# Three more pairs' first products ahead of the first feed-forward, zero matmuls in the mixer, and another order of the mixer

## The chip, the cores and the metric

The kernel runs on one core of a Trainium2 chip. The metric is the device time of one execution in microseconds, the median of several runs. Five engines take part: TensorE (PE in the profile) multiplies, VectorE (DVE), ScalarE (ACT) and GpSimd (POOL) do the elementwise work, and SyncE (SP) issues nearly all DMAs, in order.

## The reference, cut to what matters

One layer of a decoder over 1024 positions of width 1024, in float32:

```
x = x + 0.5 * swiglu(rms_norm(x), w_gate1, w_up1, w_down1)      # D_FF = 2816
h = rms_norm(x);  p = h @ w_in                                  # all columns in one projection
    8 RWKV-7 heads of 64 (token shift, decay, in-context rate, state update, group norm, gate)
    4 pooling groups of 128 (trailing means over 2, 4, 8, 16 positions, a linear map each)
x = x + concat(y_rwkv, y_pool) @ w_out
x = x + 0.5 * swiglu(rms_norm(x), w_gate2, w_up2, w_down2)
out = rms_norm(x)
```

with `swiglu(x) = (silu(x @ w_gate) * (x @ w_up)) @ w_down`.

## The kernel before, in words

**Products.** Every operand of a matmul is split into a rounded high part and a low remainder, and a product is three matmuls (`mm3`, L251 to L254: high by high, high by low, low by high), 512 columns each. One product of two 512-deep blocks is 4 steps of `mm3`, so 12 matmuls. Splitting a weight block costs one ScalarE copy (the high part) and one VectorE subtraction (the low part).

**The first feed-forward.** The gate and up projections are done as 2 by 2 blocks by a Strassen scheme with seven products P1 to P7. The 22 tiles of the inner dimension f are taken in 11 pairs. For each pair and each of the two weights (gate, up) the products P1 and P2 need only two of the seven right-hand forms, `b11` and `b21`, which are the two upper-half blocks of the normalised x itself; the others need the sums `t1` to `t4` and `b22`.

**`start` (L699 on)** is the stretch before the main loop. A planner orders it: `inputs1` loads x, transposes it, normalises it and builds all the forms, most of it on VectorE, and meanwhile PE does P1 and P2 of the first `NPRE = 3` pairs, whose sums stay in SBUF. An `aside` argument names further pairs: for these `start` also computes P1, writes it to a DRAM tile, adds P2 to it, and writes the sum to DRAM as well (L788 to L798). In this kernel only the second feed-forward passes it (pairs 8 to 10; pairs 3 to 7 of the second feed-forward are computed in the mixer, by `begin`, L1713 to L1743).

**`gate_up` (L334 on)** is the main loop over 11 pairs: it loads both 512 KB halves of a pair's weights, does what products are left, applies silu, and stores the forms of the result that the down projection wants. For a pair that was put aside it does not do P1 and P2 but loads the two kept tiles (`kept`, L443 to L448). Which pairs those are is told by `a_left`: none in the first feed-forward, all but the first three in the second.

**The mixer** (L1070 to L1909) is one list of operations for all five engines: the columns of the combined projection, eight units (four head pairs by two halves of the sequence), the pooling groups, the output projection, the norms, and `begin`. Each operation has a modelled duration and its dependences. `Plan.emit` (L95 to L169) walks through it: at each step every engine offers the operation that could start first, ties are broken by rank (the longest way to the end, plus a number per part of the list from the table `LEAD`), and what starts first is emitted. The five instruction streams that come out are final; at run time each engine goes through its stream in order and waits on semaphores. The planner knows nothing of TensorE's clock. `start` and the down projections are planned in the same way, with the same `LEAD` table.

Of the kernel before, what the change touches and what calls it, by code (L numbers as in the profile page):

```python
# [16 lines left out]
P = 128  # L17
# [5 lines left out]
HT = 512  # L23
# [12 lines left out]
class Plan:  # L36
# [51 lines left out]
    def emit(self, lead):  # L88
# [28 lines left out]
        for i in range(n):  # L117
            if not waits[i]:
                queue.setdefault(self.ops[i][0], []).append(i)
        log = []  # L120
        dense = port = 0.0
        self.span = 0.0
        while any(queue.values()):
            best = None
            for eng, q in queue.items():
                cand = []
                for i in q:
                    s = max(ready[i], clock.get(eng, 0.0) + self.turn(prev.get(eng), i), port if self.ops[i][12] else 0.0)
                    need = {}
                    for t, g in self.ops[i][4]:  # L130
                        need[g] = need.get(g, 0) + 1
                    for g, c in need.items():
                        s = max(s, sorted(free[g])[c - 1] if len(free[g]) >= c else 1e9)
                    cand.append((s, i))
                if not cand:
                    continue
                s, i = min(cand, key=lambda c: (c[0], -rank[c[1]]))
                if s > 1e8:
                    continue
                if eng == "PE" and not self.full(i) and s + self.ops[i][1] > dense + self.THIN:  # L140

                    s, i = min([c for c in cand if self.full(c[1]) and c[0] <= s + self.WAIT] or [(s, i)],
                               key=lambda c: (c[0], -rank[c[1]]))
                if best is None or s < best[0]:
                    best = (s, i, eng)
            assert best is not None, "the tiles do not suffice"
            s, i, eng = best
            _, time, fn, _, new, lat, *_ = self.ops[i]
            queue[eng].remove(i)
            end = s + time  # L150
            self.span = max(self.span, end + self.ops[i][9])
            clock[eng] = end
            prev[eng] = i
            if self.full(i):
                dense = end
            if self.ops[i][12]:
                port = max(port, end)
            for t, g in new:
                free[g].remove(min(free[g]))
            for t in tile_of.get(i, ()):  # L160
                left[t] -= 1
                ends[t] = max(ends.get(t, 0.0), end + lat)
                if not left[t] and t in tag_of:
                    free[tag_of[t]].append(ends[t])
            for u in users[i] + after[i]:
                ready[u] = max(ready[u], s if u in after[i] else end + self.lag(i, u))
                waits[u] -= 1
                if not waits[u]:
                    queue.setdefault(self.ops[u][0], []).append(u)  # L169
            log.append((s, i))  # L170
            fn()

    THIN, WAIT = 1.8, 0.2

    def full(self, i):

        return self.ops[i][0] == "PE" and self.ops[i][1] in (0.45, 0.7, 0.86)
# [7 lines left out]
    def lag(self, i, u):  # L185
# [4 lines left out]

LEAD = {"": 48.5, "1e00": 696.8, "1e01": 905.5, "1e10": -2683.6, "1e11": 2081.2, "1e20": -2679.1, "1e21": -2658.5,
# [15 lines left out]

MANUAL = {mybir.EngineType.PE, mybir.EngineType.DVE, mybir.EngineType.Activation, mybir.EngineType.Pool,  # L210
          mybir.EngineType.SP}
# [3 lines left out]
def block_kernel(ctx, tc, x, ffn1_norm, ffn1_w_gate, ffn1_w_up, ffn1_w_down, mix_norm, w_in,  # L215
# [27 lines left out]
    def split(hi, lo, src, hi_eng="act", lo_eng="dve"):  # L243
# [4 lines left out]
        eng = nc.vector if lo_eng == "dve" else nc.gpsimd  # L248
        eng.tensor_tensor(lo, src, hi.bitcast(F32), op=ALU.subtract)  # L249

    def mm3(acc, lhi, llo, rhi, rlo, first, last):  # L251
        nc.tensor.matmul(acc, lhsT=lhi, rhs=rhi, start=first, stop=False)  # L252
        nc.tensor.matmul(acc, lhsT=lhi, rhs=rlo, start=False, stop=False)  # L253
        nc.tensor.matmul(acc, lhsT=llo, rhs=rhi, start=False, stop=last)  # L254

    ident = const.tile([P, P], F32, name="ident")
    make_identity(nc, ident)
# [65 lines left out]
    NPRE = 3  # L323

    NEARLY = 5
    PROD = ("P1", "P2", "P4", "P6", "P7", "P5", "P3")
    PROD2 = ("P1", "P2", "P3", "P6", "P7", "P5", "P4")

# [2 lines left out]

    def gate_up(fp, rf, begun, wg, wu, ascr, a_left, ahead):  # L334

# [115 lines left out]
        for i in range(NF // 2):  # L451
            ahead(i)
            qs = []
            for n, src in enumerate((wg, wu)):
                a = loads(src, i) if i + n else blocks
                if (i, n) in early:
                    c1, q = early[i, n], []
                elif a_left:
                    c1, q = kept(0, i, n), [kept(1, i, n)]
                else:  # L460
                    c1, c11 = first(a)
# [234 lines left out]
        return rb  # L696


    def start(fp, rf, wg, wu, ascr, inputs, pre, through, aside=()):  # L699

# [136 lines left out]
    x_v = x[0].rearrange("(i p) d -> p i d", p=P)  # L837
    xtd = dram.tile([NH, P, KD, HT], F32, name="xtd")
    x1d = dram.tile([NH, P, KD, HT], F32, name="x1d")
    ascr = dram.tile([7, NF // 2, P, HT], F32, name="ascr")  # L840

    DSC = 4 * (16 * L + 16)
# [12 lines left out]
    with tc.tile_pool(name="f12", bufs=2, side="right", reuse_waits="tile") as fp:  # L855
# [62 lines left out]
                    else:  # L918
                        rest_ops(k, a, b, "xn0" if k == 0 else "")

        begun = start(fp, right, ffn1_w_gate[0], ffn1_w_up[0], ascr, inputs1, "1", {"PE": 4.4, "ACT": 5.8})

        wb = w_blocks(lambda n: xb.tile([P, 8 * HT], F32, tag="x", name="wx") if n == 0 else xtile("wx", [P, 8 * HT]),
                      ffn1_w_down[0], False)
# [3 lines left out]
        def mixer_consts():  # L928
# [6 lines left out]
            nc.vector.tensor_scalar(hw[:, 4:8], vt[:, vc["a0"]:vc["a0"] + 4], 0.5, None, ALU.mult)  # L935
            nc.vector.tensor_scalar(hw[:, 8:12], vt[:, vc["ka"]:vc["ka"] + 4], 0.5, None, ALU.mult)
            nc.vector.tensor_scalar(hw[:, 12:16], vt[:, vc["ka"]:vc["ka"] + 4], -0.5, 1.0, ALU.mult, ALU.add)
            reset = const.tile([P, HT], BF16, name="reset")
            nc.vector.memset(reset, 1.0)
            nc.vector.memset(reset.rearrange("p (c l) -> p c l", l=L)[:, :, 0:1], 0.0)  # L940
            inv16 = const.tile([P, 4, 16], F32, name="inv16")
# [15 lines left out]
                for q in range(3):  # L957
                    load_a(fp, 0, q, PROD)

        gate_up(fp, rf, begun, ffn1_w_gate[0], ffn1_w_up[0], ascr, False, ahead1)  # L960

        hs2 = []

# [60 lines left out]
    xbs.close()  # L1024

    x2d = dram.tile([P, KD, HT], F32, name="x2d")
    c1d = dram.tile([2, NF // 2, 2, P, HT], F32, name="c1d")
    x2n = dram.tile([NH, P, 4, D], F32, name="x2n")
    with tc.tile_pool(name="mix", bufs=1, side="right", reuse_waits="tile") as mp_:

# [29 lines left out]
        def product(name, src, c0, n, rhs, reads, r="", over="", less=0, twice=False):  # L1060


            for j in range(2):
# [39 lines left out]
                for k in range(kn):  # L1103
                    def mm(j=j, k=k, w=w, m=m):
                        rh, rl = rhs(j * KH + k)
                        mm3(E[name][0:m, :], E[f"h{w}"][:, k, 0:m], E[f"l{w}"][:, k, 0:m], rh, rl, j + k == 0,
                            j * KH + k == KD - 1)

                    op(PE, 0.7, mm, r=f"h{w} l{w} " + reads[j], w=name, group=name)
# [130 lines left out]
        def unit(u):  # L1240
# [262 lines left out]
            for c in range(NCH):  # L1503
# [16 lines left out]
                def f(c=c, cq=cq, py=py):  # L1520
                    if c % 4 == 0:
                        alloc(N(py), (aux_ps if cq else cy_ps)("py"))
                    nc.tensor.matmul(g(py)[:, c % 4 * P:(c % 4 + 1) * P], lhsT=heads(g("sv")[:, c]), rhs=heads(cm()[:, c, 1]),  # L1523
                                     start=c % 4 == 0, stop=False)
                op(PE, 0.22, f, N(f"u.r0 u.r1 u.s0{cq} u.s1{cq} sv.v0 sv.v1 {sk}"), N(py),
                   [(N(py), "ps" if cq else "cy")] if c % 4 == 0 else [])
                op(DVE, 0.2, lambda c=c: nc.vector.tensor_tensor(sb(f"z_{u}{c}", [P, P], "z", 1), E[N("pz") + f"{c}"][:, 0:P],
# [24 lines left out]
                    op(DVE, 0.5, f, N("ep") + f" ps_{u}{c} spt_{u}{c}", C if last else N(f"sv.s{c + 1}"))  # L1552

            def f():
                for c in range(NCH):
                    for h in range(2):
                        nc.tensor.matmul(g(f"py{c // 4}")[hr[h], c % 4 * P + h * L:c % 4 * P + (h + 1) * L],
# [162 lines left out]
        def begin(i, n, src):  # L1720

            c = f"fc{i}{n}"
            for d, t in enumerate(("b11", "b21")):
# [8 lines left out]
                for k in range(KH):  # L1732
                    def f(k=k, w=w, t=t, acc=acc):
                        if k == 0:
                            alloc(acc, mm_ps("pp_"))
                        mm3(E[acc], E[f"h{w}"][:, k], E[f"l{w}"][:, k], E[t][:, 0, k, :], E[t][:, 1, k, :], k == 0, k == KH - 1)
                    op(PE, 0.7, f, f"h{w} l{w} {t}.0{d * KH + k} {t}.1{d * KH + k}", acc, [(acc, "mm")] if k == 0 else [], group=acc)
                if d == 0:
# [163 lines left out]
                begin(i, n, src)  # L1902

        op(SP, 0.0, lambda: None, "prb X21")
        with tc.manual_schedule(engines=MANUAL):
            plan.emit(LEAD)
        x2 = E["X21"]
# [5 lines left out]
    with tc.tile_pool(name="f34", bufs=2, side="right", reuse_waits="tile") as fp:  # L1913
# [15 lines left out]
        def inputs2(plan, E, alloc, ct, st, sq, sub, split_op, rest_ops):  # L1929
            op = plan.op  # L1930
            for k in range(KH):
                plan.part = f"2f{k}"
                hs = []
                for m in (k, k + KH):
# [4 lines left out]
                rest_ops(k, *hs, "")  # L1939

        begun = start(fp, rf3.get, ffn2_w_gate[0], ffn2_w_up[0], ascr, inputs2, "2",
                      {"PE": 8.0, "DVE": 8.0, "ACT": 4.0, "POOL": 4.0}, range(NPRE + NEARLY, NPR))

        wb = w_blocks(lambda n: xtile("wx", [P, 8 * HT]),
                      ffn2_w_down[0], True)
# [8 lines left out]
                for q in range(3):  # L1954
                    load_a(fp, 0, q, PROD2)

        gate_up(fp, rf3, begun, ffn2_w_gate[0], ffn2_w_up[0], ascr, True, ahead2)

        fg = fp.tile([P, D], F32, tag="raw", name="fg", bufs=3)
        xo = []  # L1960
# [65 lines left out]
```

## Time and profile before

| | us |
|---|---|
| median of 3 runs (1940.72 to 1944.23) | 1943.61 |
| the profiled execution's own time | 1942.33 |
| its span, first to last instruction | 1940.6 |

| engine | busy us | share |
|---|---|---|
| PE matmul | 1841.8 | 95% |
| VectorE | 1330.0 | 69% |
| ScalarE | 816.2 | 42% |
| GpSimd | 560.6 | 29% |

The span falls into six stages: `start` of the first feed-forward (0 to about 80 us), its main loop and down projection (to about 690), the mixer (to about 1331), `start` of the second feed-forward (to about 1405), its main loop, and its down projection to the end. The page cuts the span into 40 slices and gives for each the busy share and the clock that TensorE was granted, in tenths of its full speed. A matmul at the lower level of the clock takes twice as long and counts as busy all that time, so a busy PE can still be losing time.

### The profile page before, as it was taken

How to read it: one execution, taken by the hardware profiler on the slowest of the kernel's cores; microseconds unless marked ns; L12 is line 12 of the kernel's file. 1: busy time of each engine (PE TensorE's matmuls, PEld its weight loads, DVE VectorE, ACT ScalarE, POOL GpSimd, SP SyncE). 2: the span in 40 equal slices, each digit the busy share in tenths (PEclk: the TensorE clock that was granted, in tenths of full speed). 3: DMA queues.
4: the chain of work that ended last, by engine and by line, in shares of the span. 5: the costliest groups of instructions: out<-in, count | busy, mean ns of one | idle time of the engine just before them, and what ended most of it. 6: DMA issues, size and time to landing. Idle time of an engine off the chain costs nothing.

```text
span 1940.6 us, 27950 instructions
## 1 busy us (share of the span) xinstructions
PE 1841.8 (95%) x10042; PEld 1470.9 (76%) x10042; DVE 1330.0 (69%) x2369; ACT 816.2 (42%) x1410; POOL 560.6 (29%) x519
## 2 busy tenths in 40 slices
PE   6799999999999999988899998898999999999998
PEld 5588888888888866766677777677788888888886
DVE  7865555556699867676787577465855555578976
ACT  7423233323544555355554445344432322234444
POOL 0375665552000021001310010100157678720000
PEclk9899999999999998989999999999999999999999
DMA  9344233225544333132223437325564655566333
GB/s 290 101 130 137 98 104 109 92 98 195 184 159 147 122 111 84 32 71 62 56 59 97 125 83 206 106 85 175 153 206 159 198 182 162 172 221 224 114 124 137
DMA packets 271532, 260.50 MB, mean 134 GB/s; under 512 B 68318, under 2 KB 197666, under 8 KB 271138
## 3 DMA queue, kind: packets, MB, share of 16 engines
q1 hardware_dynamic: 269952, 256.06, 42.6%
q10 hardware_dynamic: 1442, 2.66, 0.4%
q8 instruction: 80, 1.31, 0.3%
q14 instruction: 58, 0.48, 0.1%
HBM read 186.55 MB, written 71.84 MB: 133 GB/s over the span
## 4 chain that ended last, share of the span: by engine, by line
PE 45%; DVE 4%; ACT 2%; issue 1%; DMA 1%; POOL 0%; SPq 0%; POOLq 0%; ACTq 0%; DVEq 0%
PE pw L252 3%; PE pw L253 3%; PE pw L254 3%; PE pst L1541 1%; PE pz L1516 0%; DMA tscr<-ti 0%; PE py L1523 0%; PE sc L1365 0%; PE ptt L1473 0%; DVE u L1381 0%; PE pq L1473 0%; ACT L1577 0%; DMA raw<-in_ffn_w_up_dram 0%; DVE sv L1548 0%; DVE bk L1338 0%
## 5 line engine op out<-in xcount | busy, mean ns | idle before, releaser
L245 ACT ACTIVATE wf<-s 128x512 fp32r<-128x512 f32 x172 | 107.7, 631 | 289.3 <-POOL s L386 88.4
L249 DVE TENSOR_TENSOR wf<-s,wf 128x512 fp32r<-128x512 f32 x172 | 153.7, 894 | 61.4 <-ACT wf L245 59.5
L660 ACT ACTIVATE da<-ar 128x512 fp32r<-128x512 f32 x126 | 79.1, 630 | 141.8 <-PE pd__16185 L254 15.6
L249 DVE TENSOR_TENSOR wf<-raw,wf 128x512 fp32r<-128x512 f32 x76 | 78.6, 1034 | 68.6 <-ACT wf L245 67.7
L425 POOL TENSOR_TENSOR c<-c,c 128x512 f32<-128x512 f32 x60 | 98.4, 1640 | 33.6 <-DVE c L353 32.7
L392 POOL TENSOR_TENSOR s<-raw 128x512 f32<-128x512 f32 x44 | 57.2, 1300 | 144.9 <-DMA raw<-in_ffn_w_gate_dram 81.0
L663 DVE TENSOR_TENSOR da<-ar,da 128x512 fp32r<-128x512 f32 x126 | 85.8, 683 | 16.2 <-ACT da L660 16.0
L1091 DVE TENSOR_TENSOR w<-w 128x512 fp32r<-128x512 f32 (+2 forms) x108 | 70.3, 659 | 18.3 <-ACT w L1086 9.9
L1086 ACT ACTIVATE w<-w 128x512 fp32r<-128x512 f32 (+2 forms) x108 | 62.7, 595 | 47.8 <-DVE w L1091 31.3
L245 ACT ACTIVATE wf<-raw 128x512 fp32r<-128x512 f32 x76 | 47.8, 629 | 78.8 <-POOL s L403 6.2
L663 DVE TENSOR_TENSOR dw<-wx,dw 128x512 fp32r<-128x512 f32 x104 | 70.8, 683 | 9.6 <-ACT dw L660 9.6
L660 ACT ACTIVATE dw<-wx 128x512 fp32r<-128x512 f32 x104 | 64.4, 620 | 25.7 <-PE pd__5329 L254 6.9
L1995 POOL TENSOR_TENSOR s<-s,mhalf 128x1 f32<-128x1 f32 x8 | 4.7, 588 | 220.6 <-DVE s L1993 217.7
L386 POOL TENSOR_TENSOR s<-s,raw 128x512 f32<-128x512 f32 x42 | 57.0, 1357 | 33.7 <-DVE wf L249 33.0
L403 POOL TENSOR_TENSOR s<-raw,s 128x512 f32<-128x512 f32 x42 | 54.2, 1290 | 40.0 <-DVE wf L249 35.2
L252 PE MATMUL pw<-h2hi,w 128*128 128x512 f32 (+1 forms) x144 | 62.5, 434 | 2.7 <-ACT w L1086 2.7
L252 PE MATMUL pw<-h,w 128*128 128x512 f32 (+1 forms) x144 | 63.3, 440 | 0.0
L1511 ACT ACTIVATE spt<-sv,ep 128x128 f32<-128x128 f32 x60 | 24.0, 400 | 88.8 <-DVE sv L1548 79.6
L254 PE MATMUL pw<-h2hi,w 128*128 128x512 f32 (+1 forms) x144 | 59.0, 410 | 2.1 <-DVE w L1091 2.0
L409 ACT ACTIVATE c<-c 128x512 f32<-128x512 f32 x74 | 46.7, 631 | 32.9 <-DVE c L353 28.5
L384 POOL TENSOR_TENSOR s<-raw 128x512 f32<-128x512 f32 x42 | 56.6, 1349 | 8.5 <-DMA raw<-in_ffn_w_up_dram 3.0
L253 PE MATMUL pw<-h2lo,w 128*128 128x512 f32 (+1 forms) x144 | 58.4, 406 | 0.0
(3086 smaller groups left out, 5911.9 us busy)
## 6 DMA issues: line engine op xcount, KB each, us to landing
ar<-ascr SPq DMA_DIRECT2D x70, 512.0 KB
ascr<-c SPq DMA_DIRECT2D x132, 256.0 KB
raw<-in_ffn_w_gate_dram SPq DMA_DIRECT2D x44, 512.0 KB
wx<-in_ffn_w_down_dram SPq DMA_DIRECT2D x88, 256.0 KB
raw<-in_ffn_w_up_dram SPq DMA_DIRECT2D x44, 512.0 KB
w<-in_w_in_dram SPq DMA_DIRECT2D x64, 256.0 KB
ck<-c1d SPq DMA_DIRECT2D x32, 256.0 KB
w<-in_w_out_dram SPq DMA_DIRECT2D x26, 256.0 KB
```

What stands on the lines that cost most here:

```text
L245: nc.scalar.activation(hi, src, AF.Copy)
L249: eng.tensor_tensor(lo, src, hi.bitcast(F32), op=ALU.subtract)
L252: nc.tensor.matmul(acc, lhsT=lhi, rhs=rhi, start=first, stop=False)
L253: nc.tensor.matmul(acc, lhsT=lhi, rhs=rlo, start=False, stop=False)
L254: nc.tensor.matmul(acc, lhsT=llo, rhs=rhi, start=False, stop=last)
L386: nc.gpsimd.tensor_tensor(s2, s1, a11, op=ALU.subtract)
L392: nc.gpsimd.tensor_tensor(s3, a11, a21, op=ALU.subtract)
L425: eng.tensor_tensor(u[j], u[j], g[j], op=ALU.mult)
L660: nc.scalar.activation(wtile(w)[:, 0], sr(), AF.Copy)
L663: nc.vector.tensor_tensor(E[w][:, 1], sr(), E[w][:, 0].bitcast(F32), op=ALU.subtract)
L1086: nc.scalar.activation(part(t, q, kn), by32(raw), AF.Copy)
L1091: nc.vector.tensor_tensor(part(E[f"l{w}"], q, kn), by32(raw), part(E[f"h{w}"], q, kn).bitcast(F32), op=ALU.subtract)
```

## The change

It has three parts, all in one diff:

- The first feed-forward gets asides as well: `start` does P1 and P2 of pairs 3, 4 and 5 too and writes them to a new DRAM tile `c0d`, and `gate_up` reads them back. `gate_up` is now told by a range `aside` which pairs to read back.
- `Plan.emit` gets a hook: ahead of each PE operation of the mixer it looks at how long its model had PE busy in the last `TICK`; if that is under `LEAST` of it, and the operation starts after a gap, it calls `fill(n)`, which emits n matmuls of a zero weight (one bf16 column, broadcast) by the bf16 tile `reset` into the accumulator that was opened last and is not closed. They add zero to it. If nothing is open, nothing is emitted. Accumulators are entered at a product's first matmul and taken out at its last (`opened`, `closed`).
- 108 of 129 entries of `LEAD` are changed; those of the second feed-forward's `start` (`2...`) stay. The entries `1...` order the first feed-forward's `start`, the others the mixer.

```
-        log = []
+        log, worked = [], []
...
+            if eng == "PE" and self.fill:
+                t0 = s - self.TICK
+                worked = [(max(a, t0), b) for a, b in worked if b > t0]
+                gap = s - clock.get(eng, 0.0)
+                n_ = min(int((self.LEAST * self.TICK - sum(b - a for a, b in worked)) / self.FILL + 0.9), int((gap - 0.1) / self.FILL))
+                if n_ > 0 and self.fill(n_):
+                    worked.append((s - gap, s - gap + n_ * self.FILL))
+                worked.append((s, s + time))
...
+    TICK, LEAST, FILL = 3.4, 0.65, 0.22
+    fill = None
...
-LEAD = {"": 48.5, "1e00": 696.8, "1e01": 905.5, "1e10": -2683.6, "1e11": 2081.2, "1e20": -2679.1, "1e21": -2658.5,
+LEAD = {"": -264.9, "1e00": 1988.1, "1e01": 2891.4, "1e11": -36.8, "1e20": -64.8, "1e21": -450.3, "1e30": 1.9,
+        "1e31": 5.1, "1e40": 137.5, "1e41": 39, "1e50": 1846, "1e51": 742.7, "1f00": 3992.2, "1f01": 3924.3,
...
+    open_ = []
+    def opened(acc):
+        open_.append(acc)
+    def closed(acc):
+        open_[:] = [a for a in open_ if a is not acc]
...
+    reset = const.tile([P, HT], BF16, name="reset")
+    zeros = const.tile([P, 2], BF16, name="zeros")
+    nc.vector.memset(zeros, 0.0)
+    def fill(n):
+        if not open_:
+            return False
+        acc = open_[-1]
+        for _ in range(n):
+            nc.tensor.matmul(acc, lhsT=zeros[:, 0:1].to_broadcast([P, acc.shape[0]]), rhs=reset[:, 0:acc.shape[1]], start=False, stop=False)
+        return True
...
+    NASIDE = 3
...
-                elif a_left:
+                elif i in aside:
                     c1, q = kept(0, i, n), [kept(1, i, n)]
...
+    c0d = dram.tile([2, NF // 2, 2, P, HT], F32, name="c0d")
...
-        begun = start(fp, right, ffn1_w_gate[0], ffn1_w_up[0], ascr, inputs1, "1", {"PE": 4.4, "ACT": 5.8})
+        begun = start(fp, right, ffn1_w_gate[0], ffn1_w_up[0], ascr, inputs1, "1", {"PE": 4.4, "ACT": 5.8},
+                      range(NPRE, NPRE + NASIDE), c0d)
...
-        gate_up(fp, rf, begun, ffn1_w_gate[0], ffn1_w_up[0], ascr, False, ahead1)
+        gate_up(fp, rf, begun, ffn1_w_gate[0], ffn1_w_up[0], ascr, False, ahead1, range(NPRE, NPRE + NASIDE), c0d)
...
+                        if j + k == 0:
+                            E[f"a{name}"] = E[name][0:m, :]
+                            opened(E[f"a{name}"])
+                        if j * KH + k == KD - 1:
+                            closed(E[f"a{name}"])
...
+                    if c % 4:
+                        closed(E[N(py) + "a"])
+                    opened(alloc(N(py) + "a", g(py)[:, 0:(c % 4 + 1) * P]))
...
+        plan.fill = fill
         with tc.manual_schedule(engines=MANUAL):
             plan.emit(LEAD)
```

## Rows read from the trace of the kernel before

**Rows 1.** The profile page: span, busy time by engine, granted TensorE clock by slice.
```profile
span 1940.6 us, 27950 instructions
...
PE 1841.8 (95%) x10042; PEld 1470.9 (76%) x10042; DVE 1330.0 (69%) x2369; ACT 816.2 (42%) x1410; POOL 560.6 (29%) x519
...
PEclk9899999999999998989999999999999999999999
```

**Rows 2.** Windows, first `start`: stretch, length, busy by engine, PEclk, DMA share, GB/s.
```profile
0.00:20.00 20.00, 7.72 (x37) 6.54 (x37) 8.08 (x52) 13.57 (x24) 1.87 (x8) 1.00 0.91 282
20.00:60.00 40.00, 34.48 (x156) 25.08 (x157) 38.56 (x65) 27.04 (x47) 1.02 (x1) 1.00 0.71 227
60.00:80.00 20.00, 9.97 (x34) 7.41 (x34) 18.39 (x27) 7.68 (x13) 5.17 (x4) 0.74 0.38 119
```

**Rows 3.** Waits of PE, 20 to 80 us: total us, times, longest.
```profile
PE pp__613 L252 <- DVE c L792: 8.9, 1, 8.9
...
PE pp__490 L252 <- DVE c L792: 1.1, 1, 1.1
```

**Rows 4.** Timeline of VectorE at the end of that wait: start, us, line, operation.
```profile
69.03 0.68 DVE L727 TENSOR_TENSOR wf<-raw,wf 128x512 fp32r<-128x512 f32 x1
69.63 0.68 DVE L727 TENSOR_TENSOR t<-st,t 128x512 fp32r<-128x512 f32 x1
70.23 0.68 DVE L792 TENSOR_TENSOR c<-pp__562,c 128x512 f32<-128x512 f32 x1
```

**Rows 5.** Windows, second feed-forward: its `start`, then its main loop.
```profile
1340.00:1400.00 60.00, 60.00 (x255) 48.24 (x254) 58.77 (x93) 35.19 (x60) 3.69 (x3) 0.99 0.55 165
1450.00:1700.00 250.00, 250.00 (x1081) 201.35 (x1081) 142.09 (x190) 73.19 (x124) 188.86 (x133) 1.00 0.53 173
```

**Rows 6.** Tile c1d: SP's reads of kept tiles, its writes of asides.
```profile
L447 SPq DMA_DIRECT2D ck<-c1d x32: 360/431/505, 1488.6 to 1712.4; - x32
...
L796 SPq DMA_DIRECT2D c1d<-c x12: 319/338/497, 1354.1 to 1410.9; - x12
```

**Rows 7.** Windows, the mixer, and six pieces of it.
```profile
690.00:1340.00 650.00, 590.81 (x4626) 459.15 (x4625) 441.27 (x1015) 312.63 (x541) 78.36 (x143) 0.95 0.35 93
720.00:730.00 10.00, 5.88 (x45) 3.92 (x44) 7.17 (x11) 7.47 (x15) 5.79 (x7) 0.83 0.08 21
730.00:740.00 10.00, 8.09 (x27) 5.49 (x28) 9.27 (x15) 2.72 (x5) 1.49 (x2) 0.51 0.12 31
800.00:810.00 10.00, 8.89 (x89) 6.83 (x88) 7.27 (x16) 3.99 (x8) 0.00 (x0) 0.74 0.15 34
950.00:960.00 10.00, 5.38 (x117) 4.02 (x113) 7.64 (x11) 9.87 (x18) 5.54 (x8) 1.00 0.18 41
1020.00:1030.00 10.00, 10.00 (x73) 8.20 (x74) 8.12 (x18) 5.78 (x12) 0.00 (x0) 0.66 0.32 87
1220.00:1230.00 10.00, 8.74 (x151) 7.04 (x147) 7.91 (x12) 2.58 (x4) 2.54 (x2) 0.74 0.17 52
```

**Rows 8.** Waits of PE in the mixer, 690 to 1330 us.
```profile
PE ptt L1473 <- DVE bk L1480: 5.5, 6, 1.5
PE pb L1457 <- DVE bk L1338: 5.1, 4, 3.2
PE pq L1473 <- DMA bk<-tscr: 4.6, 3, 3.7
...
PE pss L1299 <- ACT t L1295: 4.0, 3, 1.5
```

**Rows 9.** Timeline of PE just ahead of a fall of the clock; idle before in brackets.
```profile
796.21 0.68 PE L1457 MATMUL pb<-ident,bk 64*128 64x64 f32 x8 [1.05 <-DVE bk L1338]
797.26 0.49 PE L1532 MATMUL pu__6575<-z,tT 128*128 128x128 f32 x2 [0.37 <-ACT tT L1492]
798.14 0.53 PE L1541 MATMUL pst<-sv,u 128*128 128x128 f32 x2 [0.39 <-DVE sv L1537]
```

**Rows 10.** The chain of waits, 1200 to 1220 us: start, us, what.
```profile
1203.20 8.56 DMA tscr<-ti
...
1215.01 3.96 DMA bk<-tscr
```

More of the change, by code (lines that the diff above doesn't have):

```diff
@@ L325, in block_kernel, with gate_up @@
     NEARLY = 5
+    NASIDE = 3
     PROD = ("P1", "P2", "P4", "P6", "P7", "P5", "P3")
     PROD2 = ("P1", "P2", "P3", "P6", "P7", "P5", "P4")
-    def gate_up(fp, rf, begun, wg, wu, ascr, a_left, ahead):
+    def gate_up(fp, rf, begun, wg, wu, ascr, a_left, ahead, aside, c1d):
         def wform(src, lo_eng):
@@ L696, in norm_bc, with start @@
         return rb
-    def start(fp, rf, wg, wu, ascr, inputs, pre, through, aside=()):
+    def start(fp, rf, wg, wu, ascr, inputs, pre, through, aside, c1d):
         plan = Plan({"raw": 3, "wf": 8, "c": 8, "cc": (2,), "st": (3,), "sq": 3, "mm": 2, "ps": 4, "ch": (1,), "cy": (1,)}, through)
@@ L839, in block_kernel @@
     x1d = dram.tile([NH, P, KD, HT], F32, name="x1d")
+    c0d = dram.tile([2, NF // 2, 2, P, HT], F32, name="c0d")
+    c1d = dram.tile([2, NF // 2, 2, P, HT], F32, name="c1d")
     ascr = dram.tile([7, NF // 2, P, HT], F32, name="ascr")
@@ L937, in mixer_consts @@
             nc.vector.tensor_scalar(hw[:, 12:16], vt[:, vc["ka"]:vc["ka"] + 4], -0.5, 1.0, ALU.mult, ALU.add)
-            reset = const.tile([P, HT], BF16, name="reset")
             nc.vector.memset(reset, 1.0)
@@ L1026, in block_kernel @@
     x2d = dram.tile([P, KD, HT], F32, name="x2d")
-    c1d = dram.tile([2, NF // 2, 2, P, HT], F32, name="c1d")
     x2n = dram.tile([NH, P, 4, D], F32, name="x2n")
@@ L1105, in mm @@
                         rh, rl = rhs(j * KH + k)
-                        mm3(E[name][0:m, :], E[f"h{w}"][:, k, 0:m], E[f"l{w}"][:, k, 0:m], rh, rl, j + k == 0,
+                        if j + k == 0:
[3 more added lines that the diff above has]
+                            closed(E[f"a{name}"])
+                        mm3(E[f"a{name}"], E[f"h{w}"][:, k, 0:m], E[f"l{w}"][:, k, 0:m], rh, rl, j + k == 0,
                             j * KH + k == KD - 1)
@@ L1554, in f @@
             def f():
+                for q in range(2):
+                    closed(E[N(f"py{q}") + "a"])
                 for c in range(NCH):
@@ L1734, in f @@
                         if k == 0:
-                            alloc(acc, mm_ps("pp_"))
+                            opened(alloc(acc, mm_ps("pp_")))
+                        if k == KH - 1:
+                            closed(E[acc])
                         mm3(E[acc], E[f"h{w}"][:, k], E[f"l{w}"][:, k], E[t][:, 0, k, :], E[t][:, 1, k, :], k == 0, k == KH - 1)
@@ L1941, in block_kernel @@
         begun = start(fp, rf3.get, ffn2_w_gate[0], ffn2_w_up[0], ascr, inputs2, "2",
-                      {"PE": 8.0, "DVE": 8.0, "ACT": 4.0, "POOL": 4.0}, range(NPRE + NEARLY, NPR))
+                      {"PE": 8.0, "DVE": 8.0, "ACT": 4.0, "POOL": 4.0}, range(NPRE + NEARLY, NPR), c1d)
         wb = w_blocks(lambda n: xtile("wx", [P, 8 * HT]),
@@ L1955, in ahead2 @@
                     load_a(fp, 0, q, PROD2)
-        gate_up(fp, rf3, begun, ffn2_w_gate[0], ffn2_w_up[0], ascr, True, ahead2)
+        gate_up(fp, rf3, begun, ffn2_w_gate[0], ffn2_w_up[0], ascr, True, ahead2, range(NPRE, NPR), c1d)
         fg = fp.tile([P, D], F32, tag="raw", name="fg", bufs=3)
```

31 rows, old and new, of the table LEAD are left out of this document.

## The prediction

> **What bounds the kernel now.** I read the page first, then the windows by stage, then who waited for whom, then single pieces of the timeline. The page says that PE is busy 1841.8 of 1940.6 us [rows 1]: whatever is to be gained lies in the 99 us in which PE idles and in the time that it runs at the lower of its two clock levels (1.2 instead of 2.4 GHz). Its clock line shows 8 only in the second slice and in two of the mixer's [rows 1], so the windows have to say where.
>
> They name two places. In the first `start` PE idles 12.3 us of the first 20, 5.5 us from 20 to 60, and 10.0 us from 60 to 80 [rows 2], while VectorE is busy 38.6 of 40 and 18.4 of 20 us: from 20 us on the stage is VectorE's, and PE has run out of products that it may do. The largest hole is one wait of 8.9 us [rows 3]: PE's next product needs the PSUM bank that an addition on VectorE frees, and that addition starts at 70.23 us, in a row of form instructions that follow one another every 0.60 us [rows 4]. Behind the hole the clock is low (0.74 over 60 to 80 us [rows 2]). In the mixer PE idles 650 − 590.8 = 59.2 us, and the mean clock is 0.95 [rows 7]. The main loops hold nothing: in the second feed-forward's, PE is busy 250.0 of 250 us at clock 1.00 [rows 5].
>
> **Part one, the asides.** Moved from the main loop to `start`: 3 pairs × 2 weights × 2 products = 12 products of 12 matmuls. A dense stretch does 1081 matmuls in 250 us [rows 5], 0.231 us each, so 144 × 0.231 = 33.3 us of PE work change place. With them go 12 splits on ScalarE and 12 on VectorE, 6 ScalarE copies and 6 VectorE additions. At 0.60 us from start to start [rows 4] VectorE gets 18 × 0.60 = 10.8 us more in the stage that it bounds: its queue ended at about 73 us and now ends at about 84.
>
> Does PE or VectorE then end the stage? Of the work up to 80 us PE has 34.5 + 10.0 = 44.5 us behind the 20 us mark [rows 2]; about 2 us of that are the lower clock's doing (4 us of matmuls there at half speed). With the 33.3 us it is 75.8 us, so without any idling PE ends at 95.8 us, after VectorE's 84. PE becomes the bound, and what is saved is idling: 5.5 + 10.0 + 2.0 = 17.5 us at most, since the 12.3 us before the first forms exist stay. I don't take all of it. The 5.5 us between 20 and 60 are waits for a split that is just being made or for a bank that is just being freed; I keep 3.5 us of them, and add 3 us for like waits of the added products (the one of 1.1 us [rows 3] is the pattern; with VectorE full, each addition that frees a bank queues behind forms). The second feed-forward's `start` has 24 products and the same two banks, and there PE is busy 60.0 of 60 us with VectorE at 58.8 [rows 5], which is why I don't take more. 17.5 − 3.5 − 3 = **11 us saved**.
>
> What it adds: 12 fetches, 12 writes and 12 later reads of 256 KB, all on SP's queue. A write occupies SP 0.34 us and a read 0.43 us [rows 6]; in `start` that is about 8 us of issuing in a queue that is also to bring x and the first weights. DMA engines are 0.91 busy in the first 20 us and 0.71 from 20 to 60 [rows 2]. If the new fetches (3.1 MB) went ahead of x at 282 GB/s [rows 2] they would delay everything by 11 us and eat the whole gain; from 60 to 80 the share is 0.38, where they and the writes fit. Read back in the main loop they cost nothing as long as SP isn't held up: the second feed-forward's loop reads 32 kept tiles [rows 6] with PE never idle [rows 5], and its GpSimd is at 188.9 of 250 us, so five-product pairs in a row are carried. Bounds of this part: −17.5 and 0.
>
> **Part two, zero matmuls.** In the mixer 14 windows of 10 us have a clock under 1, the first at 720 and the last at 1220 us [rows 7]. A window at clock c was low for 10 × (1 − c) / 0.5 us; summed over the 14 that is 54.6 us. Weighted with each window's busy share, 46.2 us of matmuls ran at half speed, so 23.1 us is the most that full clock could give. How much of that comes? First, the fills stand where the planner's model has a gap, not where the chip has one: the 8.56 us DMA in the chain [rows 10] is one that the planner counts as 2.6, so the 3.7 us wait of `pq` behind it [rows 8] gets too few. Second, nothing is filled where no accumulator is open. Third, idling and the clock don't go hand in hand: PE was busy 5.4 of 10 us from 950 to 960 and the clock stayed at 1.00, yet from 1020 to 1030 it was busy throughout at 0.66 [rows 7]. I let the fills take away half of the 23.1 us, and let two thirds of that reach the end, because VectorE is busy 441 of 650 us [rows 7] and PE's waits are on its chains [rows 8]: 23.1 × 0.5 × 0.67 = 8 us.
>
> The Trainium skill has a rule on this that speaks against the fills (TensorE: Matmul & The Clock Gate, section "HAM oscillation — how this bites in real kernels"): a clock lost in a real kernel is put down to one long wait between bursts of matmuls. By it the fills could only help behind the two long waits, and the gain would be about 2 us. This case's trace differs: the clock is down from about 798.5 us on behind idle pieces of 1.05, 0.37 and 0.39 us [rows 9], so short ones count too.
>
> The price of a fill: the trace has no bf16 matmul of this form; the nearest row is the 0.231 us of a dense 512-column one. By the code's condition a lone gap must exceed (1 − `LEAST`) × `TICK` = 1.2 us before it gets a fill; the waits with longest pieces of 3.7, 3.2 and 1.5 us [rows 8] are of that kind, eleven pieces in all, and with clusters of short ones I estimate 70 fills, 16 us of PE. In true gaps they cost nothing; if all 70 met a PE that had work ready, 16 us. I take 2 us. Net **6 us saved**; bounds −23 and +16.
>
> **Part three, the order.** New weights change no operation and no duration; they redraw where 59 us of idling fall. One item is plainly one of order: the `pq` wait of 4.6 us [rows 8] behind DMAs that took 8.56 and 3.96 us [rows 10], while PE had nothing to put in between. I take **3 us saved** for such an item. Bounds: half of the idling away, −30; on the other side the third rival below, +32.
>
> **Sum.** The profiled execution took 1942.33 us (span 1940.6 and 1.7 around it), 1.3 us under the median of the runs, 1943.61. 1942.3 − 11 − 6 − 3 = 1922.3: **1922 us**.
>
> **Rivals.**
> 1. *All of it works*: asides 17, fills 15, order 10, so 1942 − 42 = 1900 us. For it: 23.1 us at half clock and 59.2 us of idling are there to take [rows 7]. Against it: PE's waits in the mixer are dozens of pieces under 1.5 us on VectorE chains [rows 8], and these don't go by reordering.
> 2. *Only the asides count*: the zero matmuls don't hold the clock (wrong place, nothing open, or zeros don't do it) and cost 2 us, and the order is neutral: 1942 − 11 + 2 = 1933 us. For it: 950 to 960 against 1020 to 1030 [rows 7]; the skill's section above would give nearly the same.
> 3. *Slower by the order of the units*: each of the eight units sends its small inverse through DRAM and back before `pq` may start. At 1203 to 1219 us that way was laid open: 4.6 us of waiting [rows 8], then a stretch at clock 0.74, 5.2 us low [rows 7], of which half of 87% is lost, 2.3 us; with `pt` and `ptt` waiting behind it (1 us each) about 8 us. If the new order puts too little ahead of `pq` in four further units, that is +32: 1942 − 11 + 32 − 6 (fills as forecast) = 1957 us. From about two such units on, 17 us, the change is no gain. Against it: the other seven units show waits of `pq` of 0.9 us together [rows 8].
> 4. *Nothing to see*: one or two such units, or fetches of asides ahead of x (up to 11 us), against the gains: 1940 to 1947 us.
>
> **How the numbers follow.** Differences under 0.2%, 3.9 us, can't be told from no change here: faster is under 1939.7 us, slower over 1947.5. Chances: the forecast (1908 to 1930) 0.48, rival 1 (below 1908) 0.13, rival 2 (1930 to 1939.7) 0.17, rival 4 0.10, rival 3 0.12. Faster 0.48 + 0.13 + 0.17 = 0.78, same 0.10, slower 0.12. A range from 1900 to 1946 leaves out rival 3, half of rival 1 and a little of rival 4, about 0.20; the forecast's own is 1908 to 1930.
>
> **What would show it.** Part one: from 60 to 80 us PE near 20 of 20 at clock 1.00, the 8.9 us wait gone, 12 reads of `c0d` in the main loop with PE still 50 of 50; wrong if PE's idling before 60 us grows, or if waits for DMA appear ahead of the first products. Part two: a line of bf16 matmuls in the mixer, and clock 1.00 in nearly all its windows; wrong if the low stretches stand beside the fills. Part three: waits of `pq` and PE's idling in the mixer below 59 us; wrong if `pq <- DMA` grows. The prediction falls if the mixer, now about 641 us from 690 to 1331, is longer than before, whatever the first stage does.

## The result, and the profile after

The changed kernel takes 1897.48 us (median of 4 runs, 1895.34 to 1899.51) beside 1943.12 for the kernel before: 45.6 us less, ratio 0.9767 [0.975, 0.9783]. The forecast was 1922, the range 1900 to 1946; the sign was right, the size was half. Its profiled execution has a span of 1895.3 us. The first view is the page (answers to [rows 1]).

```profile
span 1895.3 us, 28104 instructions
...
PE 1825.0 (96%) x10101; PEld 1459.2 (77%) x10108; DVE 1329.2 (70%) x2370; ACT 811.7 (43%) x1410; POOL 568.5 (30%) x519
...
PEclk9999999999999999999999999999999999999999
```

The three 8s of the clock line are gone. The windows of the first `start` and of the mixer follow (answers to [rows 2, 7]; stretch, length, busy time of PE, PE's weight loads, VectorE, ScalarE and GpSimd, clock, DMA share, GB/s).

```profile
0.00:20.00 20.00, 10.71 (x54) 8.93 (x55) 8.99 (x55) 15.25 (x27) 1.87 (x8) 1.00 0.95 311
20.00:60.00 40.00, 38.51 (x181) 30.59 (x180) 34.88 (x57) 25.00 (x44) 1.99 (x1) 1.00 0.84 255
60.00:80.00 20.00, 18.23 (x72) 14.25 (x71) 17.00 (x28) 10.73 (x21) 0.00 (x0) 0.91 0.72 243
...
670.50:1289.00 618.50, 576.39 (x4669) 446.00 (x4674) 437.04 (x1011) 309.05 (x535) 88.12 (x166) 0.99 0.36 95
```

PE's idling from 20 to 80 us fell from 15.5 to 3.3 us, and already in the first 20 us PE does 3.0 us more. From 60 to 80 us PE is busy 18.2 of 20 us at clock 0.91, not quite the "near 20 of 20 at clock 1.00" that the prediction named as its sign. The wait of 8.9 us [rows 3] is gone; the longest one left there is of 1.8 us:

```profile
PE pp__643 L274 <- DVE c L830: 1.8, 1, 1.8
```

Three landmarks give the stages: the first matmul of a mixer product, the last write of a `c1d` tile by the mixer, and the end. Before they lie at 691.7, 1332.1 and 1940.6 us, after at 670.7, 1288.5 and 1895.3. So the first feed-forward lost 21.0 us, the mixer 22.6 (640.4 to 617.8), the rest 1.7. In the mixer the zero matmuls are there, 59 in the matmul records, nearly all into `py` (66 by their weight loads, so a few matmul records are missing), and the 12 reads of kept tiles cost PE nothing (350.0 of 350 us busy from 100 to 450 us):

```profile
L288 PE MATMUL py<-reset,zeros x55: 219/272/527, 744.8 to 1177.1; 128*128 128x128 bf16 x25, 128*128 128x256 bf16 x13, 128*128 128x384 bf16 x12, 128*128 128x512 bf16 x5
L288 PE MATMUL pw<-reset,zeros x4: 379/379/392, 713.2 to 1075.4; 128*128 128x512 bf16 x4
```

```profile
L485 SPq DMA_DIRECT2D ck<-c0d x12: 360/454/507, 175.1 to 251.8; - x12
```

Half-clock time in the mixer, summed over windows of 2 us as (1 − clock) × 2 / 0.5, is 54.6 us before and 13.6 after.

### The profile page after: what moved, and what is told of

It reads as the page before. It is cut to its first block, busy times and chain, and to the rows that moved or that the text cites. A ratio compares the mean times of both kernels' runs of the same rounds, so it can differ in the third digit from the quotient of the medians.

```text
span 1895.3 us, 28104 instructions
## 1 busy us (share of the span) xinstructions
PE 1825.0 (96%) x10101; PEld 1459.2 (77%) x10108; DVE 1329.2 (70%) x2370; ACT 811.7 (43%) x1410; POOL 568.5 (30%) x519
## 3 DMA queue, kind: packets, MB, share of 16 engines
q1 hardware_dynamic: 279744, 265.50, 45.5%
## 4 chain that ended last, share of the span: by engine, by line
PE 87%; DVE 5%; ACT 3%; DMA 2%; issue 1%; SPq 0%; POOL 0%; POOLq 0%; DVEq 0%; ACTq 0%
PE pw L274 5%; PE pw L276 5%; PE pw L275 5%; PE pz L1561 1%; PE pst L1589 1%; PE sc L1410 1%; PE py L1568 1%; PE ptt L1518 1%; PE pq L1518 0%; PE pt L941 0%; DVE u L1426 0%; DMA xn<-in_x_dram 0%; DMA c0d<-c 0%; DMA xtd<-sq 0%; PE pb L1502 0%
## 5 line engine op out<-in xcount | busy, mean ns | idle before, releaser
L263 DVE TENSOR_TENSOR wf<-s,wf 128x512 fp32r<-128x512 f32 x172 | 164.1, 954 | 78.9 <-ACT wf L259 77.8
L263 DVE TENSOR_TENSOR wf<-raw,wf 128x512 fp32r<-128x512 f32 x64 | 65.3, 1021 | 64.1 <-ACT wf L259 63.5
L441 POOL TENSOR_TENSOR s<-raw,s 128x512 f32<-128x512 f32 x42 | 54.9, 1307 | 31.0 <-DVE wf L263 31.0
L259 ACT ACTIVATE wf<-raw 128x512 fp32r<-128x512 f32 x64 | 40.1, 626 | 51.8 <-PE pp__12669 L276 4.1
```

The lines of the kernel that those rows point to most:

```text
L259: nc.scalar.activation(hi, src, AF.Copy)
```

## The experiments

Every kernel was timed in five rounds beside the kernel before, whose median was 1941.9 to 1943.2 us in the five sets. An interval is about ±0.2%, 3 to 4 us.

### Order and zeros, each alone (e1 to e3)

e1 takes the zeros out of the changed kernel:

```
-        plan.fill = fill
```

> The changed kernel without its 59 zero matmuls; order, asides and everything else as in it. Theory 'the fills hold the clock': in the mixer the half-clock time goes back from 13.7 us towards the 54.6 us of before, some 30 us more of it, half of that lost: 1910 us (1905 to 1915). Rival 'the new order holds the clock, the fills are ornament': half-clock time stays under 20 us and the time is 1894 to 1900 us, perhaps 1 to 2 us under the changed kernel's 1897.5 because 59 matmuls are gone.

Measured: 1902.0 us, ratio 0.98 [0.9777, 0.9822], between the ranges of theory and rival. e2 and e3 put the old weights of the mixer back (all keys but `1...`), with and without zeros:

```
-LEAD = {"": -264.9, "l0": 100.5, "u0": 77.2, ...
+LEAD = {"": 48.5, "l0": -66.5, "u0": -73.4, ...
```

> The changed kernel with the mixer's old weights (start of the first feed-forward new, with asides), zero matmuls on. Theory 'fills': the old order with fills loses about 15 of its 54.6 us of half clock's 23 us: mixer of 641 - 12 = 629 us, time 1908 us. Rival 'order': the mixer stays at 639 to 643 us, time 1918 to 1922 us. If the new order alone is worth the whole 22.5 us, this kernel is where the first stage's gain shows by itself: 1943 - 21 = 1922 us.

Measured: 1912.2 us, 0.9853 [0.9831, 0.9874], again between the two ranges.

> The changed kernel with the mixer's old weights and no zero matmuls: only the first stage (asides and its new weights) differs from the kernel before. Both theories: mixer as before, 641 us, first feed-forward 21 us shorter as in the changed kernel's trace: 1922 us (1919 to 1925). If it comes out at 1930 or more, what the first stage gained is partly given back later; if at 1915 or less, the mixer gains by starting from another state.

Measured: 1919.9 us, 0.9889 [0.987, 0.9907]. The mixers of the three traces, one row each for e3, e2 and e1 (columns as above):

```profile
672.10:1311.00 638.90, 582.05 (x4609) 452.64 (x4607) 438.70 (x1011) 309.68 (x535) 77.86 (x140) 0.96 0.35 92
```

```profile
670.00:1302.80 632.80, 586.04 (x4687) 450.61 (x4689) 438.57 (x1011) 309.37 (x535) 79.33 (x140) 0.98 0.35 93
```

```profile
669.70:1295.60 625.90, 580.37 (x4609) 451.75 (x4607) 437.23 (x1011) 308.82 (x535) 89.48 (x163) 0.96 0.36 94
```

| kernel | order, zeros | median us | mixer us | PE idle | half clock |
|---|---|---|---|---|---|
| before | old, none | 1943.1 | 640.4 | 54.9 | 54.6 |
| e3 | old, none | 1919.9 | 638.9 | 56.9 | 47.8 |
| e2 | old, 78 | 1912.2 | 632.8 | 46.8 | 23.9 |
| e1 | new, none | 1902.0 | 625.9 | 45.5 | 47.7 |
| changed | new, 59 | 1897.5 | 617.8 | 41.6 | 13.6 |

(Mixer from the first product to the last `c1d` write; idle is that length minus PE's busy time; half clock is the time at the lower clock.) Read down the table: the first stage alone is worth 1941.95 − 1919.9 = 22.0 us (1941.95 is the median of the kernel before in that set); the zeros are worth 7.7 us with the old order and 4.5 with the new; the order is worth 14.7 us with zeros and 17.9 without. 22.0 + 7.7 + 14.7 = 44.4; that this is nearly the 45.6 is no proof, since each step starts where the last one ended. By the lengths of the mixers in single traces the zeros are worth 6.1 and 8.1 us, the order 15.0 and 13.0; so the two readings of a term differ by up to 5 us.

The 4.5 us alone would be inside the intervals, but the half-clock time isn't: both pairs of kernels differ in nothing but the zeros, and it falls from 48 to 24 and from 48 to 14 us. The new order without zeros has as much half clock as the old, so the order alone holds no clock: both rivals on that are out. Without zeros the order saves idling, 11.4 of the 13.0 us. With zeros on, only 5.2 us of the 15.0 are idling (46.8 to 41.6); the other 9.8 are busy time of PE, by fewer zero matmuls (16.0 to 12.2 us) and less half clock (23.9 to 13.6 us).

### Where the new order idles less (e13 to e16)

PE's idling ahead of `pq`, `pt` and `ptt` (the refinement of the units' inverse), for e3 and then e1: who ended it, us, times.

```profile
  DVE bk L1523: 9.2, 10
  DMA bk<-tscr: 4.7, 2
  ACT sy L1624: 1.7, 1
```

```profile
  DVE bk L1531: 1.6, 2
  DVE bk L1525: 1.0, 2
  ACT sy L1626: 0.8, 1
  DMA bk<-tscr: 0.5, 1
```

15.6 against 3.9 us: 11.7 us, as much as all the idling that went. That looked like the cause. The test (cut here to one operand; it leaves the refinement out of the result) gives `pt` and `ptt` another operand, which is always ready, in the same order, without zeros:

```
-   lambda r, c: ch(q_())[r, c, :]                      # pt's right, ptt's left operand
+   lambda r, c: bones[r, L - r.start:P - r.start]      # a block of zeros
```

> The kernel of e1 (new order, no zeros) in which pt and ptt read a constant block of zeros in place of the masked pq, so they don't wait for VectorE's masking; the refinement of the inverse is left out of the result by that, the instructions and their order are the same. New order: those waits were 1.6 us in all, so little is gained: 1898 to 1902 us (e1: 1902.0).

> The same edit in the kernel of e3 (old order, no zeros). Theory 'the new order's gain is that PE no longer stands waiting ahead of pt and ptt': 9.2 us of waits go and the time falls from 1919.9 to some 1911 us (1909 to 1913), so that the two orders are 9 to 11 us apart instead of 17.9. Rival 'these waits only stand beside it, and PE then waits elsewhere': 1916 to 1920 us, the two orders still 15 us or more apart.

Measured: 1902.6 us, 0.9789 [0.9773, 0.9806], and 1919.0 us, 0.988 [0.9866, 0.9893]. The waits for the masking are gone from e14's trace, and the time is not: 16.4 us still lie between the orders. PE's idling fell by 4.7 us only (56.9 to 52.2), and half clock rose to 64.9 us. To be rid of the clock's part, the second pair has zeros on, and takes away the DMA's waits too (`pq`'s and `tT`'s operands replaced in the same way):

> The kernel of e2 (old order, zeros on) in which pq, pt and ptt read a constant block of zeros instead of what comes from DRAM and from VectorE's masking: PE waits for nothing of the inverse there; the inverse's refinement is left out of the result, instructions and order are the same. Theory 'the new order's gain is PE not waiting there': some 12 of the 15 us of waits are gained, 1912.2 - 12 = 1900 us (1898 to 1904). Rival 'PE only waits further on, where the inverse is used (pu) or for the next unit': 1909 us or more.

> The same edit in the changed kernel (new order, zeros on), which waits there 5.7 us. Theory and rival alike: 1894 to 1897.5 us. What tells them apart is the distance between the two orders, 14.7 us without the edit: under 7 us by the theory, 12 us or more by the rival.

Measured: 1908.0 us, 0.9824 [0.9805, 0.9844], and 1897.0 us, 0.9766 [0.9749, 0.9784]. By the medians the distance between the orders is 11.0 us in place of 14.7, nearer to the rival, and the 3.7 us between are inside the intervals. By the mixers of the traces it is 7.7 us (626.9 and 619.2) in place of 15.0, nearer to the theory, but the clock is in that: half clock is 17.1 us in e15 (23.9 in e2) and 20.5 in e16 (13.6 in the changed kernel). By PE's idling it is 3.7 us (43.1 and 39.4) in place of 5.2. e15's waits show where some of them went (e2 waited 14.6 us ahead of these matmuls, and 4.5, 2.4, 2.8 and 1.6 us at the four places shown):

```profile
PE pss L1342 <- ACT t L1338: 5.2, 3, 2.2
...
PE pw L272 <- ACT w L1124: 4.7, 4, 1.9
PE pst L1587 <- DVE sv L1583: 3.5, 6, 0.9
...
PE pw L274 <- DVE w L1129: 2.2, 4, 1.0
```

12.9 us of waits were taken away, 5.9 us of mixer went (632.8 to 626.9), and PE's idling fell by 3.6. So 9.3 us came back, 4.3 of them at these four places (waits for a square, for a split and for the state), the rest in smaller pieces. The rival thus holds for the larger part of these waits. How much of the order's 15 us they are, anything from 1.5 to 7 us by the reading chosen, isn't settled; for the rest no single wait was shown, and its cause stays open.

### Parts of the order (e9 to e11)

The table of weights (given here as a rule; in the kernels it is written out), new for the eight units and old for the rest of the mixer; the reverse; and old for the first half of the sequence, new for the rest:

```
-LEAD = {...}                                       # all new
+LEAD = {k: (NEW if k[0] == "u" else OLD)[k] ...}   # e9; e10 the other way round; e11 by halves
```

> The changed kernel with the mixer's weights new for the eight units alone (u0 to u7), old for everything else in the mixer. Theory 'the units' weights take the way through DRAM off PE's path': PE's waits of ptt, pt and pq fall as in the changed kernel and the time is 1897 to 1901 us. Rival 'it is the weights of what fills the gaps (projections, pooling, the second feed-forward's first products)': 1910 to 1914 us, as with the old mixer and zeros (1912.2). Second rival 'the weights only work as a set': 1908 us or more here and in the next run.

> The reverse: the mixer's old weights for the eight units, new ones for everything else. Theory 'units': 1910 to 1914 us, with ptt waiting for VectorE some 5 us and pq for its DMA some 4 us as before. Rival 'fillers': 1897 to 1901 us. Second rival 'only as a set': 1908 us or more.

> The changed kernel with old weights for the mixer's first half of the sequence (l0, u0 to u3, p00 to p03, n1) and new ones for the rest. By the traces without zeros, PE's idling differs most from 1170 to 1220 us (8.9 us with old weights, 3.0 with new): theory 'the gain lies in the last units': 1902 to 1905 us, more than half of the 14.7 us kept. Rival 'it is spread over all units': 1905 to 1909 us.

Measured: 2011.1 us, 1.035 [1.0336, 1.0364]; 2014.1 us, 1.0365 [1.0351, 1.0379]; 2034.3 us, 1.0465 [1.0445, 1.0485]. None came near its theory; "only as a set" holds, and far more strongly than it was put: the mixed tables take 99 to 122 us more than the whole old table with zeros (e2). The weights are added to the rank that decides ties, so a part's place depends on all others. The zeros were on in all three and didn't rescue them: from the first product to the second `start`'s first write of an aside, 754 to 777 us (655 in e2), PE idles 97 to 102 us (51) and the clock is low for 99 to 140 us (31), with 267 to 309 weight loads of zeros (82). A gain can't be read off single entries, and a mixed table can cost over three times the 32 us that the prediction gave it as the upper bound.

### Asides and the start's order (e4 to e8, e12)

```
-    NASIDE = 3
+    NASIDE = 0      # e4; e5: 1, e6: 2
```

> The changed kernel with no pair put aside (P1 and P2 of pairs 3 to 5 back in the main loop), the start's new weights and the mixer as in it. Theory 'asides fill PE's idling behind VectorE': the idle piece from 60 to 75 us comes back, only what the earlier x loads give stays (about 3 to 5 us): 1897.5 + 16 = 1913 us. Rival 'the start's new order does most of it': 1900 to 1904 us.

Measured: 1916.2 us, 0.9866 [0.9847, 0.9885].

> The changed kernel with one pair put aside instead of three. Theory 'what is saved is PE's idling behind VectorE': without asides the first stage is 16.6 us longer; each pair brings PE 11.1 us of work and VectorE 3.6 us, so 16.6 - 7.5 = 9.1 us are left with one: 1897.5 + 9 = 1906.5 us (1904 to 1909). Rival 'each pair gives the same third of 18.7 us': 1910 us.

Measured: 1910.6 us, 0.9835 [0.9822, 0.9849].

> The changed kernel with two pairs put aside instead of three. Theory 'idling behind VectorE': 16.6 - 2 x 7.5 = 1.6 us left: 1899 us (1896.5 to 1901). Rival 'each pair the same third': 1904 us.

Measured: 1903.5 us, 0.9799 [0.9785, 0.9812]. By the medians the rival is right, 5.5, 7.2 and 6.0 us a pair. By the stage itself (the start of the first mixer product) the theory is: 687.3, 681.3, 673.1 and 670.7 us with none to three pairs, so 16.6, 10.6 and 2.4 us left, where e4's 16.6 led to a forecast of 9.1 and 1.6. (The same first stage ends between 668.1 and 672.1 us in the twelve kernels that share it, so the 2.4 is inside the scatter and the 10.6 isn't.) The rest of the difference lies in the mixers, whose instruction streams are the same: 620.4, 622.7, 621.9 and 617.8 us, with 17.1, 27.3, 17.1 and 13.6 us at half clock. Without asides the hole is back, a wait of 12.2 us (e4, PE from 18 to 100 us):

```profile
PE pp__615 L276 <- DVE wf L765: 12.2, 1, 12.2
```

e8 keeps three asides but orders the start by the old weights, with 500 for each of the asides, which the old table doesn't have:

```
-"1e00": 1988.1, "1e01": 2891.4, ... "1e30": 1.9, ... "1x0": 2992.2
+"1e00": 696.8, "1e01": 905.5, ... "1e30": 500, ... "1x0": 1680.9
```

> The changed kernel with the old weights for the first feed-forward's start; its six groups of asides get 500 each. Theory 'asides need no new order': only the 3.3 us of the earlier x loads are lost: 1901 us (1899 to 1903). Rival 'the order has to make room for them': fetches and banks of the asides push the forms back, and half or more of the 18.7 us goes: 1908 us or more.

Measured: 1914.4 us, 0.9856 [0.9842, 0.987]: the rival. The stage ends at 685.8 us, 15.1 later than with the new weights; 10.7 us of that are idling of PE (23.3 us of it in the stage beside 12.6). Its waits are the small ones for a bank that the prediction had counted on, and others of the kind:

```profile
PE pp__525 L272 <- ACT c L826: 2.1, 1, 2.1
...
PE pp__638 L272 <- ACT c L826: 1.2, 1, 1.2
...
PE pp__495 L272 <- DVE c L828: 1.0, 1, 1.0
...
PE pp__709 L272 <- DVE c L828: 0.8, 1, 0.8
```

So the asides pay in full only in an order that has room for them: the order alone gives 4.4 us (691.7 to 687.3), the asides in the old order 5.9 (to 685.8), both together 21.0. (Other weights for the asides in the old order weren't tried.) What the order does by itself is seen in the first 10 us. Before, SP issues weights ahead of x, after, x first; SP's first issue and PE's first transpose, before and after:

```profile
0.81 1.00 SPq L783 DMA_DIRECT2D raw<-in_ffn_w_up_dram  x2
...
8.29 0.48 PE L900 MATMUL pt<-ident,xn 128*128 128x128 f32 x1 [3.94 <-DMA xn<-in_x_dram]
```

```profile
0.81 1.82 SPq L913 DMA_DIRECT2D xn<-in_x_dram  x4
...
5.14 0.47 PE L941 MATMUL pt<-ident,xn 128*128 128x128 f32 x1
```

### More of both (e7, e12)

```
-    TICK, LEAST, FILL = 3.4, 0.65, 0.22
+    TICK, LEAST, FILL = 3.4, 0.9, 0.22
```

> The changed kernel with LEAST 0.90 instead of 0.65, so that zero matmuls are put into shorter gaps too. Theory 'they hold the clock': the half-clock time in the mixer falls from 13.7 to under 8 us and the time by 1 to 2 us, to about 1896 us. Rival 'they are in the way': their number doubles, PE reaches its next operation later, and the time rises to 1900 us or more at the same clock.

Measured: 1894.8 us, 0.9753 [0.974, 0.9767]; 132 zero matmuls in place of 59, half clock 10.3 us in place of 13.6, the mixer 617.9 us. The theory's "under 8 us" wasn't reached, and the number doubled without the rival's harm. There is no gain that the intervals tell apart from the changed kernel's 0.9767.

> Four pairs put aside and LEAST 0.90. With three pairs PE idles 3.3 us behind the first 20 us, and that is all that a fourth pair can fill; theory 'idling behind VectorE': 0 to 3 us under the 1894.8 us of LEAST 0.90 with three pairs, so 1892 to 1895 us. Rival 'each pair the same 6 us', as the medians of none to three pairs run: 1889 us.

Measured: 1894.8 us, 0.9762 [0.9743, 0.9782]. A fourth pair gives nothing: the stage ends at 670.0 us, with three pairs (e7) at 669.5. That fits the stage's reading above, not an even 6 us a pair. Neither of the two is shown to beat the changed kernel.

## Why the prediction was wrong

The forecast took 20 us off (11, 6 and 3); the runs gave 44.4 (22.0, 7.7 and 14.7). Of the 24 us between, 11.0 lie in part one and 11.7 in part three. These two steps failed.

- **What bounds the kernel** was right: the gain came from the two places that the windows named, and the main loops gave nothing.
- **Part one, mis-sized** (11 us taken; 22.0 measured). Two terms failed. "The 12.3 us before the first forms exist stay": they don't, the new weights bring x ahead of the weight blocks and take 3.0 us there, 4.4 us of the stage. The diff shows the `1...` weights changed, and the text ahead of the prediction says what they order, yet they were priced at nothing. And the 3.5 + 3 us kept back for waits on splits and banks: from 20 to 80 us the changed kernel idles 3.3 us in all, while with the old order 10.7 us are left (e8). So such waits come with the order, not with the asides. Without these 6.5 us the bound of 17.5 us stands beside 16.6 in the stage and 18.7 in the medians. That PE and not VectorE would bound the stage was right; so, roughly, was the sum by which each pair leaves 7.5 us less (11.1 us of PE work less 3.6 of VectorE's; 10.6 and 2.4 us left, against 9.1 and 1.6).
- **Part two, right in size** (6 us taken; 4.5 with the new order, 7.7 with the old). The number of zeros was forecast at 70, there are 66. (The "eleven pieces" behind the 70 don't come out of [rows 8], where the four waits have 16 pieces, many too short to get a fill.) By its reasoning half of the half-clock time was to go, and two thirds of the matmul time saved by that was to reach the end. With the old order half went (47.8 to 23.9 us), at most 12 us of matmul time, and 7.7 us reached the end. With the new one some seven tenths went (47.7 to 13.6 us), at most 17 us, and only 4.5 by the medians, 8.1 by the mixer: there two errors of opposite sign meet, which is luck.
- **The rule of the Trainium skill that spoke against it** (TensorE: Matmul & The Clock Gate, "HAM oscillation — how this bites in real kernels", one long wait between bursts) does not describe this mixer: e1's trace is low for 47.7 us with no wait of PE in the mixer over 2.9 us. The Trainium skill's next section on that page ("A second HAM failure mode: psum-queue depth-cycling", where short idle pieces between groups of matmuls make the clock swing) is nearer to it, though here the pieces are waits for other engines.
- **Part three, the other step that failed** (3 us taken; 14.7 to 17.9 measured). "They redraw where 59 us of idling fall" was right, and then only one visible item, `pq`'s wait for its DMA, was given to the order. That item went as taken, from 4.6 us [rows 8] to 1.3:

```profile
PE pq L1518 <- DMA bk<-tscr: 1.3, 1, 1.3
```

  All else that the order gave, some 12 us, had no term in the sum. The bound of −30 was in the text; no row tells where between −30 and +32 an order lies, and the value was set near zero because one item could be named. Without zeros the idling fell by 11.4 us over many waits. Which of them make the gain stays open: taking those of `pq`, `pt` and `ptt` away in the old order gave 4.2 us (e15), about the width of the intervals.
- **The rivals.** What came is the first, "all of it works" (1900 us, chance 0.13), with other shares: asides and start 22, order 15 to 18, zeros 4.5 to 7.7, where it had 17, 10 and 15. The slower rival was possible in kind: mixed tables cost 68 to 92 us over the kernel before (e9 to e11), through the whole mixer and not through `pq` alone.

## What to carry to other kernels

When a diff contains a new table of priorities, price each stage that the table orders, the first one too, and give the order a wide share: in this kernel it was the largest single term that the trace of before could not show. A stage's idling behind another engine is a good bound for work moved into it, and the bound is reached where the order makes room; take the stage's own end from the trace to judge it, since the total also carries some 5 us by which equal mixers differ from trace to trace. A wait that vanishes between two traces is not yet the cause: take it away in the other order and see whether the time follows, in the idling as well as in the total.

## What the runs showed of the hardware that was not expected

- One mixer, instruction for instruction the same on PE, took 617.8 to 622.7 us in four kernels (e4 to e6 and the changed one), the longer the more half clock it had, 13.6 to 27.3 us. The moment at which it starts differs; whether that or chance decides isn't shown, for runs of the changed kernel alone lie 4.2 us apart.
- The bf16 weight loads of the zeros take half the time of the products' loads: 98 ns beside 188 ns for the projections' high parts (both 128 columns; min/median/max, in the changed kernel's trace). The zeros are one column read 128 times, so whether the number type or the reading makes the difference isn't shown.

```profile
L288 PEld LDWEIGHTS <-zeros x66: 96/98/152, 708.0 to 1177.1; 128*128 128x128 bf16 x66
```

```profile
L274 PEld LDWEIGHTS pw<-h2hi,w x144: 159/188/330, 670.4 to 933.9; 128*128 128x128 f32 x136, 128*96 128x96 f32 x8
```

- Products of zeros count for the clock: with 59 of them in the records, some 12 us of PE, half clock falls from 47.7 (e1) to 13.6 us. They don't make up for a bad order: see e9 to e11.
